# A decoder layer with 32 experts on one core: big tiles in one block by hand, another order of the front, and expert weights in pieces of 16 KB

## The chip, the cores and the metric

One core of one Trainium2 chip runs the kernel; all arithmetic is float32. The core's engines are PE (TensorE, matrix products; its weight loads are listed as PEld), DVE (VectorE), ACT (ScalarE), POOL (GpSimd) and SP (SyncE, which issues most DMAs). 16 DMA engines move the data. The metric is the time of one execution on the device in microseconds (us), the median of the runs. The profile is of one execution; its times count from the span's start, and "L122" is line 122 of the kernel.

## The reference: what is computed

One layer over 256 tokens of 1024 features:

```
proj = x @ w_in                               # 1024 -> 768 + 256
y_mix = s5_mixer(proj[:, :768])               # 48 groups of 16, 64 complex states each; GELU; GLU gate with w_glu
y_mem = cross_attention(proj[:, 768:], mem @ mem_w_k, mem @ mem_w_v)    # 4 heads, 256 memory rows
h  = layer_norm(2**0.25 * x + concat(y_mix, y_mem) @ w_out)
for each token: its 4 best of 32 experts by h @ router_w + router_b, gates = softmax of the 4 logits
expert e: g, l = split(h @ w_gu[e] + b_gu[e]);  g = min(g, 7);  l = clip(l, -7, 7)
          y_e = (g * sigmoid(1.702 * g) * (l + 1)) @ w_down[e] + b_down[e]
out = layer_norm(2**0.25 * h + sum of gate * y_e)
```

w_gu[e] is 1024 x 2048 and w_down[e] 1024 x 1024: 8.39 and 4.19 MB for each of the 32 experts, 402.65 MB in all.

## The kernel before

**The front.** x and w_in are loaded and x is transposed (xT). The S5 mixer is computed in chunks of eight tokens: DVE works out the powers of the state matrix from the small parameters (`apw`, put into PSUM as `tab`), and the function `power` (L439) forms from them three tiles m1p (input side) and three tiles m2 (output side, m20 to m22): two products on DVE into a tile and into `ptmp`, and their sum on POOL. `mats` (L214) transposes the parameters b and c from their raw layouts (`rawb`, `rawc`) for this. Out of m1p PE makes kb and, transposed by kc, the tiles tz: the products inside a chunk. ACT fills tz by copies (two from each PSUM bank of kc, and five that shift rows, for each of three blocks). u is the mixer's input; it goes through DRAM once (`ud`) to change its layout to u_sb. The state at the start of each chunk comes from a scan on DVE (`@SC1`: the rotated input through `tensor_tensor_scan`, real and imaginary part, and `@SC2`: rotated back into xs), with the table wsc that DVE builds by doubling (`@W`). `yb` sums the products inside the chunk (`@Yt`, u_sb by tz) and from the states (`@Yx`, xs by m2). Then follow GELU (`@GEL`), transposes to yT, the gate (`zp`, products with w_glu) and ymT.

Beside it runs cross-attention: mem is transposed (memT), qps, kps and vmp are the three projections, sc the scores, prob the softmax on ACT, pT its transposes and pv the product, copied to ymem (a part of `att`). `out_mem` multiplies ymem with the last quarter of w_out, and the loop at L885 multiplies ymT with the rest; all of it sums up in the four PSUM banks yp[i][hf] (i is a half of the tokens, hf a half of the features). q counts eight slices of 128 rows of w_out; slices 2 and 3 are done over all four banks, slices 4 to 7 (QO = 4) bank by bank. DVE adds the residual and takes the norm's sums, POOL raises the variance to the power -0.5, DVE normalizes, and `affine` applies gain and offset (POOL, and DVE for the last quarter). The router follows for each half i: hTp transposes, `logits`, `chosen` (the four best), ranks.

**The experts.** For expert e, `gather` (L984) makes a 0/1 matrix `oh` from ranks and multiplies the columns of h_sb (stationary, 128 of them at a time) with it: xg holds up to 64 tokens of the expert, transposed. `up` (L1014) runs eight steps kt with 128 rows of w_gu each; `act` is the clamped SwiGLU; `act_t` (L1035) transposes it in four pieces; `down` (L1044) multiplies with w_down; every second expert `combine` adds both experts' rows to `acc` by their gates. On PE the order in an expert is up, combine (every second), gather of the next expert, act_t, bias of the next, down. What would not fit in 64 slots is done by two `If` blocks behind (L1255, L1293); with these inputs they do nothing.

**Memory and loads.** A pool `big` has 22 tiles of 128 x 2048 f32 (1 MB each); a tile is handed out again when its last reader is done, and everything large lives there, weights too. `load_gu` loads 128 rows of w_gu (row kt * 128 + p to partition p, 8 KB in one piece) into one tile, `load_down` 256 rows of w_down (two pieces of 4 KB to a partition). SP issues them in the order written; an issue waits until its tile is free. Expert 31's last tile comes in two halves. At e = 22 two tiles are taken for b_down (`bd`) and the last norm's vectors.

**Order.** Instructions of PE, DVE and ACT are pinned to the order of the program (`pin`, L97; the class `Ordered`, L108). POOL and the DMA issues of SP are not: the scheduler may move them where their inputs are ready. The markers `dbg("@...")` do nothing.

Of the kernel before, what the change touches and what calls it, by code (L numbers as in the profile page):

```python
# [9 lines left out]
F32 = mybir.dt.float32  # L10
# [6 lines left out]
P = 128  # L17
# [10 lines left out]
MISS = 8192.0  # L28
NBIG = 22
# [11 lines left out]
def kernel(  # L41
# [35 lines left out]
    big = ctx.enter_context(tc.tile_pool(name="big", bufs=NBIG))  # L77
# [4 lines left out]

    def big_tile(name):
        return big.tile([P, 2048], F32, tag="big", name=name)
# [23 lines left out]
    class Ordered:  # L108
# [5 lines left out]
        def __getattr__(self, name):  # L114
            f = getattr(self.eng, name)
            return f if name == "dma_start" else lambda *a, **k: pin(f(*a, **k))  # L116

    S = Ordered(S)
    V = Ordered(V)

# [37 lines left out]
    SP.dma_start(x_sb[:, 0, :], x[0, 0:P, :])  # L158
    SP.dma_start(ldt, log_dt.rearrange("(g o) -> g o", o=1))
    SP.dma_start(araw[:, 0, :], a_re)  # L160
    SP.dma_start(araw[:, 1, :], a_im)
    SP.dma_start(x_sb[:, 1, :], x[0, P : 2 * P, :])
    win = []
    for k2 in range(4):
        t = big_tile(f"win_{k2}").rearrange("p (k n) -> p k n", k=2)
        for k in range(2):
            kt = 2 * k2 + k
            SP.dma_start(t[:, k, :], w_in[kt * P : (kt + 1) * P, :])
            win.append(t[:, k, :])
# [29 lines left out]
    )  # L199
    tt(dsk, dsk, same.unsqueeze(1).to_broadcast([P, 12, NH]), ALU.mult, G)  # L200
# [13 lines left out]
    def mats(name, in_of, a_of, b_of):  # L214
        t = big_tile(name)
        pad.append(t[:, 0 : 768 + NH])
        o = [t[:, 784 * k : 784 * k + 768].rearrange("p (g h) -> p g h", h=NH) for k in range(2)]
        for h8 in range(2):
            ps = bank(f"{name}p{h8}")
            for hh in range(8):  # L220
                tr(ps[:, NG * hh : NG * hh + NG], in_of(8 * h8 + hh), ident[0:NG, 0:NG])
            v = ps[:, 0 : 8 * NG].rearrange("p (h g) -> p g h", h=8)
            hs = slice(8 * h8, 8 * h8 + 8)
            a_of(o[0][:, :, hs], v)
            for q in range(2):
                pq, pr = slice(64 * q, 64 * q + 64), slice(64 - 64 * q, P - 64 * q)
                b_of(o[1][pq, :, hs], v[pr], pq)
        return o
# [26 lines left out]
    for kt in range(KT):  # L255
        for q in range(6):
            mm(
                ups[q // 2][:, NT * (q % 2) : NT * (q % 2) + NT], win[kt][:, P * q : P * q + P], xT[:, kt, :],
                kt == 0 and q % 2 == 0, kt == KT - 1, True,
            )  # L260
        if kt == 1:
            rbv = rawb.rearrange("g q p h -> g (q p) h")
            ba, bb_ = mats("bab", lambda h: rbv[:, :, h], lambda o, v: S.copy(o, v), lambda o, v, pq: S.copy(o, v))
        if kt == 3:
            ca, cb = mats(
                "cab", lambda h: rawc[:, h].rearrange("g q p -> g (q p)"),
                lambda o, v: S.mul(o, v, sgc), lambda o, v, pq: S.mul(o, v, sgc[pq]),
            )
            ca_pad = pad[1]
            G.memset(ca_pad[:, 768:784], 0.0)  # L270
    dbg("@LWO", None)
    wo = []
    ov = w_out[0, 0:MIX, :].rearrange("(j r) n -> r j n", r=192)

    def load_wo(k2):
        t = big_tile(f"wo{k2}").rearrange("p (k n) -> p k n", k=2)
        if k2 == 3:
            SP.dma_start(t, w_out[0, MIX:D, :].rearrange("(k p) n -> p k n", p=P))
        elif k2 < 2:
            SP.dma_start(t, ov[0:P, 2 * k2 : 2 * k2 + 2, :])  # L280
        else:
            op = ov[P:192].rearrange("r (q e) n -> e r q n", e=2)
            for e in range(2):
                SP.dma_start(t[64 * e : 64 * e + 64], op[e])
        return [t[:, 0, :], t[:, 1, :]]

    wo += load_wo(3)
# [116 lines left out]

    tab = [bank("tab0")[:, 0 : (Q + 1) * NG], bank("tab1")[:, 0 : (Q + 1) * NG]]
# [9 lines left out]
    for q in range(2):  # L415
        S.copy(bbb[64 * q : 64 * q + 64], bba[64 - 64 * q : P - 64 * q])
    dbg("apw", apw)

    dbg("@LD", None)
    mem_sb = big_tile("mem_sb").rearrange("p (m d) -> p m d", m=2)  # L420
    SP.dma_start(mem_sb, mem[0].rearrange("(m p) d -> p m d", p=P))
    wk = big_tile("wk").rearrange("p (k n) -> p k n", k=KT)
    SP.dma_start(wk, mem_w_k.rearrange("(k p) n -> p k n", p=P))
    wv = big_tile("wv").rearrange("p (k n) -> p k n", k=KT)
    SP.dma_start(wv, mem_w_v.rearrange("(k p) n -> p k n", p=P))
# [13 lines left out]
    def power(name, j, k0, m):  # L439
# [9 lines left out]
        tt(o, o, ptmp[j % 2], ALU.add, G)  # L449
# [6 lines left out]
    m1p = groups(m1p_t)  # L456

# [8 lines left out]

    dbg("@W", None)

    wsc = big_tile("wsc")
    w_re, w_im = wsc[:, 0:768], wsc[:, 768:1536]  # L470
    wre, wim = (t.rearrange("p (r c) -> p r c", c=NC) for t in (w_re, w_im))
    cv, mv_ = small("cv", (P, 2, 24)), small("mv_", (P, 24))
    for a in range(2):
        pa = slice(64 * a, 64 * a + 64)
        for o, src in ((cv[pa, 0], cs), (cv[pa, 1], sn), (mv_[pa], mag)):
            G.tensor_copy(o, src[pa].rearrange("p (r a) -> p a r", a=2)[:, a])
    e_, f_ = small("e_", (P, 2, 24)), small("f_", (P, 2, 24))
    r8 = small("r8", (P, 24, NC))
    r8f = r8.rearrange("p r c -> p (r c)")
    us = [  # L480
        u.rearrange("p (r c) -> p r c", c=NH)
        for u in (wsc[:, 1536:1920], small("u4", (P, 384)), r8f[:, 0:384], r8f[:, 384:768])
    ]
    s4 = [small(f"s4{k}", (P, 24)) for k in range(4)]

    def cmul4(o_re, o_im, x_re, x_im, y_re, y_im, t):
        yield tt(t[0], x_re, y_re, ALU.mult)
        yield tt(t[1], x_im, y_im, ALU.mult)
        yield tt(t[2], x_re, y_im, ALU.mult)
# [12 lines left out]
    while n < NC:
        b_ = [cur[:, q].unsqueeze(2).to_broadcast([P, 24, n]) for q in range(2)]
        together(
            cmul4(
                wre[:, :, n : 2 * n], wim[:, :, n : 2 * n], wre[:, :, 0:n], wim[:, :, 0:n], b_[0], b_[1],
                [u[:, :, 0:n] for u in us],
            ),
            sq(nxt, cur) if 2 * n < NC else iter(()),
        )  # L510
        n, cur, nxt = 2 * n, nxt, cur

    for _ in range(3):
        tt(mv_, mv_, mv_, ALU.mult)
# [29 lines left out]
    dbg("@KM", None)  # L544

    proj("kps", kT, lambda q, kt: wk[:, kt, P * q : P * q + P], lambda q, kt: memT[:, kt, :], (0,))
    dbg("@LG1", None)
    wgl += load_wgl(1)
    dbg("@K", None)

    kr_t = big_tile("kr")
    kr = kr_t[:, 0 : 12 * 144].rearrange("p (b n) -> p b n", b=12)
    G.memset(kr[:, :, 0:NH], 0.0)
    tz = []
    for b in range(3):
        tz.append(big_tile(f"tz{b}"))
        G.memset(tz[b], 0.0)
# [10 lines left out]
    tt(kr[:, :, NH : 2 * NH], kr[:, :, NH : 2 * NH], dsk, ALU.add, G)  # L568
# [12 lines left out]
    dbg("@M2A", None)  # L581
    m2 = groups([power("m20", 0, 1, (ca, cb))])
# [748 lines left out]
```

## Time and profile before

| what | value |
|---|---|
| median of 3 runs (lowest, highest) | 1109.77 us (1107.32, 1111.62) |
| the profiled execution | 1110.52 us, its span 1108.8 us |
| PE busy | 1056.9 us, 95% of the span |
| PE weight loads busy | 487.9 us, 44% |
| DVE, ACT, POOL busy | 285.5, 153.0, 55.6 us |
| moved by DMA | 424.75 MB, mean 383 GB/s |
| packets | 89016; under 8 KB 56180 |
| w_gu loads | 256 of 1024 KB, 19.9 us from issue to landing |
| w_down loads | 127 of 1024 KB, 20.1 us from issue to landing, and 2 of 512 KB |
| mean granted PE clock | 0.989 of full |

How to read it: matmuls are pipelined, and PE counts as busy while one is under way, so 95% does not say that PE is the limit. Which engine ends last is in the chain of waits, which is followed back from the last instruction. Where DMA loads are queued, the 20 us from issue to landing are mostly queue.

### The profile page before, as it was taken

What the parts mean: (1) busy time and instruction counts of PE and PEld (TensorE: products, weight loads), DVE (VectorE), ACT (ScalarE), POOL (GpSimd) and SP (SyncE); (2) the same over time, 40 slices, a digit from 0 to 9 for tenths busy, and PEclk for the clock granted to TensorE, in tenths of its full rate; (3) what the DMA queues carried; (4) which work ended last, traced back from release to release, by engine and by line L of the source; (5) the groups of instructions that cost most, each with busy time, mean ns of one, the idle gap of its engine ahead of it and who ended that gap; (6) DMA issues with size and microseconds to landing.
All of it is one profiled execution on the core that took longest, in us unless ns stands there. A gap on an engine that the chain in (4) does not pass through costs nothing.

```text
span 1108.8 us, 13702 instructions
## 1 busy us (share of the span) xinstructions
PE 1056.9 (95%) x5733; PEld 487.9 (44%) x5733; DVE 285.5 (26%) x632; ACT 153.0 (14%) x288; POOL 55.6 (5%) x56
## 2 busy tenths in 40 slices
PE   9988999999999999999999898989899998999994
PEld 8875654444444444444443343434243433444331
DVE  7976151121212121212121112121021212121104
ACT  4484120000000000000000000000000000011002
POOL 1750030000000000000000000000000000000001
PEclk9998999999999999999999999999999999999998
DMA  8948969999999999999999999999999999999992
GB/s 230 240 139 274 408 258 408 417 415 416 414 416 416 416 415 416 417 416 417 416 417 415 415 416 416 416 416 415 400 417 416 416 416 416 415 417 416 415 406 82
DMA packets 89016, 424.75 MB, mean 383 GB/s; under 512 B 15902, under 2 KB 18866, under 8 KB 56180
## 3 DMA queue, kind: packets, MB, share of 16 engines
q1 hardware_dynamic: 88660, 423.27, 96.1%
q8 instruction: 48, 0.79, 0.3%
q10 hardware_dynamic: 288, 0.52, 0.1%
q14 instruction: 20, 0.16, 0.0%
HBM read 421.93 MB, written 1.84 MB: 382 GB/s over the span
## 4 chain that ended last, share of the span: by engine, by line
PE 58%; DMA 37%; ACT 2%; DVE 1%; SPq 1%; issue 1%; ACTq 0%; POOL 0%; DVEq 0%
PE gu_e L122 24%; DMA gu_e<-in_exp_w_gu_dram 22%; PE dn_e L122 13%; DMA dn_e<-in_exp_w_down_dram 13%; PE xgp_e L122 7%; PE cb_e L122 4%; PE yp L122 3%; DMA win<-in_l_w_in_dram 1%; PE zp L122 1%; ACT tz L116 1%; PE atp_e L125 1%; DMA mem_sb<-in_mem_dram 1%; PE qps L122 1%; PE kps L122 1%; ACT prob L116 1%
## 5 line engine op out<-in xcount | busy, mean ns | idle before, releaser
L122 PE MATMUL gu_e<-gu_e,xg_e 128*64 128x512 f32 x2048 | 458.0, 597 | 27.0 <-DMA gu_e<-in_exp_w_gu_dram 26.3
L122 PEld LDWEIGHTS gu_e<-gu_e,xg_e 128*64 128x64 f32 x2048 | 141.9, 137 | 336.9 <-issue 253.0
L122 PE MATMUL dn_e<-dn_e,xl_te 128*64 128x512 f32 x1024 | 226.8, 595 | 0.8 <-ACT xl_te L116 0.7
L122 PEld LDWEIGHTS dn_e<-dn_e,xl_te 128*64 128x64 f32 x1024 | 70.6, 137 | 154.2 <-issue 127.7
L1028 DVE TENSOR_SCALAR xl_e<-gu_e 128x512 f32<-128x512 f32 x32 | 22.1, 692 | 430.5 <-PE gu_e L122 430.5
L122 PEld LDWEIGHTS xgp_e<-oh_e,h_sb 128*128 128x128 f32 x1024 | 118.1, 192 | 7.3 <-issue 4.3
L122 PE MATMUL xgp_e<-oh_e,h_sb 128*128 128x64 f32 x1024 | 118.2, 273 | 0.0
L1056 DVE COPY y_e<-dn_e 64x512 f32<-64x512 f32 x32 | 21.9, 684 | 252.8 <-PE dn_e L122 252.8
L116 ACT ACTIVATE sg_e<-xl_e 128x512 f32<-128x512 f32 x32 | 20.2, 630 | 405.6 <-DVE xl_e L1028 405.6
L122 PE MATMUL cb_e<-y_e,ogT_e 128*128 128x512 f32 x120 | 55.8, 604 | 0.0
L116 ACT COPY y_e<-dn_e 64x512 f32<-64x512 f32 x32 | 18.6, 582 | 257.4 <-DVE y_e L1056 250.2
L116 ACT COPY xg_e<-xgp_e 128x512 f32<-128x512 f32 x32 | 18.8, 586 | 155.5 <-PE xgp_e L122 155.5
L128 DVE TENSOR_TENSOR acc<-acc,cb_e 128x512 f32<-128x512 f32 x56 | 36.2, 681 | 6.6 <-PE cb_e L122 6.6
L122 PEld LDWEIGHTS cb_e<-y_e,ogT_e 128*128 128x128 f32 x120 | 21.6, 190 | 32.6 <-issue 29.7
L122 PE MATMUL gu_e<-bgu,ident 32*64 32x512 f32 x256 | 34.8, 612 | 0.0
L1125 POOL MEMSET bd<- 128x1280 f32 x1 | 1.2, 1165 | 583.4 <-PE gu_e L122 583.4
L131 DVE TENSOR_SCALAR oh_e<-iota,rk 128x64 f32<-128x64 f32 x62 | 12.9, 252 | 66.7 <-PE xgp_e L122 66.7
L1030 DVE TENSOR_SCALAR xr_e<-gu_e 128x512 f32<-128x512 f32 x32 | 22.1, 692 | 3.1 <-PE gu_e L122 0.2
L1031 DVE SCALAR_TENSOR_TENSOR xr_e<-xr_e,xl_e 128x512 f32<-128x512 f32 x32 | 22.0, 688 | 0.5
L122 PE MATMUL ups<-xT,win 128*128 128x256 f32 x96 | 21.7, 383 | 0.5 <-DMA win<-in_l_w_in_dram 0.5
L1032 DVE TENSOR_TENSOR xr_e<-xr_e,sg_e 128x512 f32<-128x512 f32 x32 | 21.9, 686 | 0.6 <-DVE og_e L131 0.2
L122 PE MATMUL yp<-wo,ymT 128*128 128x512 f32 x48 | 20.9, 594 | 0.0
(286 smaller groups left out, 594.8 us busy)
## 6 DMA issues: line engine op xcount, KB each, us to landing
gu_e<-in_exp_w_gu_dram SPq DMA_DIRECT2D x256, 1024.0 KB, 19.9
dn_e<-in_exp_w_down_dram SPq DMA_DIRECT2D x127, 1024.0 KB, 20.1
win<-in_l_w_in_dram SPq DMA_DIRECT2D x8, 512.0 KB, 11.0
wo<-in_w_out_dram SPq DMA_DIRECT2D x3, 1024.0 KB, 5.7
wgl<-in_l_s_w_glu_dram SPq DMA_DIRECT2D x2, 768.0 KB, 8.3
x_sb<-in_x_dram SPq DMA_DIRECT2D x2, 512.0 KB, 4.4
mem_sb<-in_mem_dram SPq DMA_DIRECT2D x1, 1024.0 KB
wk<-in_mem_w_k_dram SPq DMA_DIRECT2D x1, 1024.0 KB
```

Source lines behind the costliest of these rows:

```text
L116: return f if name == "dma_start" else lambda *a, **k: pin(f(*a, **k))
L122: pin(PE.matmul(o, lhsT, rhs, start=start, stop=stop, skip_group_check=shared))
L125: pin(PE.transpose(o, in_, ident if idn is None else idn))
L128: return (eng or V).tensor_tensor(out=o, in0=x0, in1=x1, op=op)
L131: return (eng or V).tensor_scalar(out=o, in0=x0, scalar1=s1, scalar2=s2, op0=op0, op1=op1)
L1028: V.tensor_scalar(out=xl_, in0=ps[0], scalar1=7.0, scalar2=None, op0=ALU.min)
L1030: V.tensor_scalar(out=xr, in0=ps[1], scalar1=7.0, scalar2=-7.0, op0=ALU.min, op1=ALU.max)
L1031: V.scalar_tensor_tensor(out=xr, in0=xr, scalar=1.0, in1=xl_, op0=ALU.add, op1=ALU.mult)
L1032: V.tensor_tensor(out=xr, in0=xr, in1=sg, op=ALU.mult)
L1056: eng(y[:, 512 * dh : 512 * dh + 512], ps[dh][64 * dh : 64 * dh + 64, :])
L1125: G.memset(t[:, 0:width], 0.0)
```

## The change

`big` becomes one tile of 22 slots of 2048 columns; a table `slot_of` gives each large tile of the front its slot by hand, two or more in turn in one slot. The experts' weights have a ring of blocks of two slots (ROWS = 2, 16 KB in one piece to a partition): ten blocks in slots 0 to 19, taken in the order 0 to 7, then 9, then 8. A w_gu load brings rows t * 256 + 2p and 2p + 1 to partition p (2 MB, four per expert), a w_down load rows t * 512 + 4p to 4p + 3 (2 MB, two per expert). To match, `gather` reads every second column of h_sb, and `act_t` every fourth column of the activation. SP's instructions, its DMA issues too, are now pinned to the order of the program. Expert 31's last block comes in pieces of two, one and one rows.

In the front: the small parameters are issued by ACT; the second half of x is issued right behind the first; mem, mem_w_k and mem_w_v are loaded early; rawc has another layout (q before h), and c gets its layout by matmuls with the identity instead of transposes, 2 x 2 small ones for each h; ACT's copies of it (`take_c`) come after tab and bbt. `m20` and `m21` are formed right after m1p, and m21, m22 and kr are added on DVE and not on POOL; the scan's decays r8 are made on POOL. The order of the sections changes as below. The transposed h (hT) leaves the large tiles.

```
before: ... M1A (m1p) MT UL W XQ KM K(kb, kr) M1B(m1tp) M2A KM1 SIN M2B SM(sc) kc,tz M2C SMb(max, exp) SMr
        SC1 VM VM1 PV1 SC2 Yt out_mem(1) out_mem(0) Yx GEL Z(yT) zp ...
after:  ... M1A M2(m20, m21) MT UL XQ K(kb, kr) M2C(m22) W(to 16) KM kc,tz0 KM1 SM SMb(max) W(32) tz1 M1B SIN
        exp VM VM1 SC1(real) tz2 SMr SC1(imag) Yt PV1 LX LXG SC2 Yx out_mem(1) GEL Z(yT) out_mem(0) zp ...
```

```diff
-    big = ctx.enter_context(tc.tile_pool(name="big", bufs=NBIG))
+    big = ctx.enter_context(tc.tile_pool(name="big", bufs=1)).tile([P, NBIG * 2048], F32, tag="big", name="big")
+    slot_of = {}
+    for k, names in enumerate((
+        "ptmp0 wsc", "ptmp1 gt", "m20", "m21", "m22", "u_sb", "cab s_in tw yg", "memT xs", "bbt wo3", "bab att",
+        "mem_sb wgl0", "wk wgl1", "x_sb m1p1 wgl2", "xT prob yT", "rawb m1p2 wo0", "rawc m1p0 wo1", "win_2 tz1 gb",
+        "win_3 tz2", "win_0 sv wo2", "win_1 tz0 ymT", "wv h_sb", "ut kr pT x2 acc",
+    )):
+        for name in names.split():
+            slot_of[name] = k
     def big_tile(name):
-        return big.tile([P, 2048], F32, tag="big", name=name)
+        k = slot_of[name]
+        return big[:, 2048 * k : 2048 * (k + 1)]
+    ring = [2 * k + n for k in (0, 1, 2, 3, 4, 5, 6, 7, 9, 8) for n in range(0, 2, ROWS)]
+    def next_block():
+        ring.append(ring.pop(0))
+        return big[:, 2048 * ring[-1] : 2048 * (ring[-1] + ROWS)]
...
+    SP = Ordered(SP)
...
-        tt(o, o, ptmp[j % 2], ALU.add, G)
+        tt(o, o, ptmp[j % 2], ALU.add, eng)
...
+    m2 = [power("m20", 0, 1, (ca, cb)), power("m21", 1, 1, (ca, cb), V)]
...
-    tt(kr[:, :, NH : 2 * NH], kr[:, :, NH : 2 * NH], dsk, ALU.add, G)
+    tt(kr[:, :, NH : 2 * NH], kr[:, :, NH : 2 * NH], dsk, ALU.add)
...
-    QO = 4
+    QO = 6
...
+    hv = h_sb.rearrange("p i (t r j) -> p i t j r", r=P, j=ROWS)
-                    ps[:, CAP * kt : CAP * kt + CAP], h_sb[:, i, kt * P : (kt + 1) * P], oh[:, i, :],
+                    ps[:, CAP * kt : CAP * kt + CAP], hv[:, i, kt // ROWS, kt % ROWS], oh[:, i, :],
...
+        av = a.rearrange("s (c p j) -> s c j p", p=P, j=2 * ROWS)
-            tr(ps[:, P * c : P * c + P], a[:, P * c : P * c + P])
+            tr(ps[:, P * c : P * c + P], av[:, c // (2 * ROWS), c % (2 * ROWS)])
...
-    def load_gu(n, src, kt):
-        t = big_tile(f"gu{kt}_{n}")
-        SP.dma_start(t, src[kt * P : (kt + 1) * P, :])
-        return t
+    def load_gu(src):
+        w = []
+        for t in range(KT // ROWS):
+            b = next_block().rearrange("p (j n) -> p j n", j=ROWS)
+            SP.dma_start(b, src[t * ROWS * P : (t + 1) * ROWS * P, :].rearrange("(p j) n -> p j n", j=ROWS))
+            w += [b[:, j, :] for j in range(ROWS)]
+        return w
...
+    def load_down(src, split=False):
+        n, w = 2 * ROWS, []
+        for t in range(KT // n):
+            b = next_block().rearrange("p (j n) -> p j n", j=n)
+            rows = src[t * n * P : (t + 1) * n * P, :].rearrange("(p j) n -> p j n", j=n)
...
         if e == NE - 10:
+            k = ring[0]
+            slot_of.update(bd=k, gb2=k, rows2=k + 1, o=k + 1)
+            del ring[0 : 2 // ROWS]
```

## Rows read from the trace of the kernel before

**Rows 1.** The page, part 2: GB/s that the DMA engines moved, in 40 slices of 27.7 us.
```profile
GB/s 230 240 139 274 408 258 408 417 415 416 414 416 416 416 415 416 417 416 417 416 417 415 415 416 416 416 416 415 400 417 416 416 416 416 415 417 416 415 406 82
```

**Rows 2.** The chain of waits in order of time: start us, us, what.
```profile
160.78 13.95 PE gu_e L122 x64
...
213.23 13.73 PE gu_e L122 x64
...
268.68 13.73 PE gu_e L122 x64
...
548.91 20.16 DMA dn_e<-in_exp_w_down_dram
...
1047.56 1.94 PE gu_e L122 x8
...
1065.12 8.58 PE gu_e L122 x40
```

**Rows 3.** Windows: length, busy us of each engine (instructions), granted PE clock, DMA share, GB/s.
```profile
30.00:40.00 10.00, 7.72 (x37) 6.85 (x36) 10.00 (x6) 5.24 (x7) 8.96 (x4) 0.83 1.05 374
...
620.00:624.00 4.00, 3.41 (x13) 1.16 (x12) 1.91 (x3) 0.63 (x1) 0.00 (x0) 1.00 1.02 409
632.00:644.00 12.00, 12.00 (x58) 4.02 (x56) 0.68 (x1) 0.58 (x1) 0.00 (x0) 1.00 1.01 420
...
1082.00:1087.00 5.00, 4.10 (x19) 1.66 (x19) 1.39 (x3) 0.96 (x2) 0.00 (x0) 1.00 0.46 181
...
540.00:1060.00 520.00, 493.67 (x2494) 200.67 (x2492) 92.59 (x186) 44.33 (x81) 2.12 (x2) 1.00 1.02 415
```

**Rows 4.** Timeline of SP's queue up to 215 us: start us, us, engine, line, issue, output and input.
```profile
2.67 0.42 SPq L162 DMA_DIRECT2D x_sb<-in_x_dram  x1
...
155.24 11.31 SPq L1088 DMA_DIRECT2D dn_e<-in_exp_w_down_dram  x4
167.90 17.88 SPq L1081 DMA_DIRECT2D gu_e<-in_exp_w_gu_dram  x8
```

**Rows 5.** Groups of PE weight loads: shapes, count, busy us, mean ns, idle before.
```profile
L122 PEld LDWEIGHTS xgp_e<-oh_e,h_sb 128*128 128x128 f32 x1024 | 118.1, 192 | 7.3 <-issue 4.3 <-PE cb_e L122 2.9
...
L125 PEld LDWEIGHTS babp<-ident,rawb 48*128 48x128 f32 x16 | 1.8, 203 | 0.3 <-issue 0.3
...
L125 PEld LDWEIGHTS cabp<-ident,rawc 48*128 48x128 f32 x16 | 1.1, 139 | 0.3 <-issue 0.3
```

**Rows 6.** Timeline of PE in the front: start us, us, instruction, count, idle time before it.
```profile
35.54 3.45 PE L125 MATMUL memT<-ident,mem_sb 128*128 128x128 f32 x16 [2.28 <-DMA mem_sb<-in_mem_dram]
...
49.44 2.83 PE L122 MATMUL kb<-m1p,cab 128*32 128x128 f32 x96
...
72.69 0.66 PE L125 MATMUL kc<-ident,kr 128*128 128x128 f32 x4 [2.42 <-ACT tz L116]
...
84.14 4.08 PE L125 MATMUL pTp<-ident,prob 128*128 128x128 f32 x16 [2.19 <-ACT prob L116]
88.91 3.68 PE L122 MATMUL pv<-pT,att 128*64 128x256 f32 x16 [0.69 <-ACT pT L116]
...
109.81 15.96 PE L122 MATMUL zp<-yT,wgl 128*128 128x256 f32 x96
125.69 20.87 PE L122 MATMUL yp<-wo,ymT 128*128 128x512 f32 x48
...
150.79 1.09 PE L125 MATMUL hTp<-ident,x 128*128 128x128 f32 x8
```

**Rows 7.** Timeline of DVE in the front.
```profile
39.67 5.24 DVE L116 TENSOR_TENSOR s<-cv 128x24 f32<-128x24 f32 x4
...
98.74 1.89 DVE L116 TENSOR_TENSOR xs<-tw 64x744 f32<-64x744 f32 x2
```

**Rows 8.** Timeline of ACT in the front.
```profile
76.78 3.13 ACT L116 COPY tz<-tz 32x512 f32<-32x512 f32 x5
```

**Rows 9.** Timeline of POOL in the front.
```profile
143.02 2.59 POOL L128 TENSOR_TENSOR h_sb<-x,gb 128x512 f32<-128x512 f32 x2 [0.80 <-issue]
```

More of the change, by code (lines that the diff above doesn't have):

```diff
@@ L214, in mats @@
     def mats(name, in_of, a_of, b_of):
[L215 to L217 removed]
+        banks = []
         for h8 in range(2):
@@ L287, with project @@
-    wo += load_wo(3)
+    def project(k0, k1):
+        for kt in range(k0, k1):
+            for q in range(6):
+                mm(
+                    ups[q // 2][:, NT * (q % 2) : NT * (q % 2) + NT], win[kt][:, P * q : P * q + P], xT[:, kt, :],
+                    kt == 0 and q % 2 == 0, kt == KT - 1, True,
+                )
+    project(0, 2)
+    rbv = rawb.rearrange("g q p h -> g (q p) h")
+    ba, bb_ = mats("bab", lambda h: [rbv[:, :, h]], lambda o, v: S.copy(o, v), lambda o, v, pq: S.copy(o, v))()
@@ L288 @@
+    project(2, 4)
+    take_c = mats(
+        "cab", lambda h: [rawc[:, q, h] for q in range(2)], lambda o, v: S.mul(o, v, sgc), lambda o, v, pq: S.mul(o, v, sgc[pq]),
+    )
+    project(4, 8)
     dbg("@par", None)
@@ L403 @@
         )
+    cv, mv_ = small("cv", (P, 2, 24)), small("mv_", (P, 24))
+    for a in range(2):
+        pa = slice(64 * a, 64 * a + 64)
+        for o, src in ((cv[pa, 0], cs), (cv[pa, 1], sn), (mv_[pa], mag)):
+            G.tensor_copy(o, src[pa].rearrange("p (r a) -> p a r", a=2)[:, a])
+    for _ in range(3):
+        tt(mv_, mv_, mv_, ALU.mult, G)
+    r8 = small("r8", (P, 24, NC))
+    G.tensor_copy(r8, mv_.unsqueeze(2).to_broadcast([P, 24, NC]))
+    G.memset(r8[:, :, 0], 0.0)
     tab = [bank("tab0")[:, 0 : (Q + 1) * NG], bank("tab1")[:, 0 : (Q + 1) * NG]]
@@ L543 @@
     wgl += load_wgl(0)
[L544 to L548, printed above, removed]
+    wo += load_wo(3)
     dbg("@K", None)
+    tz = [big_tile(f"tz{b}") for b in range(3)]
+    for t in tz:
+        G.memset(t, 0.0)
     kr_t = big_tile("kr")
@@ new lines @@
+    dbg("@LG1", None)
+    wgl += load_wgl(1)
+    dbg("@SM", None)
+    scores = []
+    for i in range(2):
+        sc = [bank(f"sc{i}{e}") for e in range(2)]
+        for h2 in range(2):
+            for e in range(2):
+                pe = slice(64 * e, 64 * e + 64)
+                mm(
+                    sc[e][:, NT * h2 : NT * h2 + NT], xqT[pe, h2, i * P : (i + 1) * P], kT[pe, h2, :],
+                    True, True, True,
+                )
+        scores.append(sc)
+    dbg("@SMb", None)
@@ new lines @@
+    prob = big_tile("prob").rearrange("p (i h m) -> p i h m", i=2, h=4)
+    sums = []
+    for i, sc in enumerate(scores):
+        mx, sm = small(f"mx{i}", (P, 4)), small(f"sm{i}", (P, 4))
+        for e in range(2):
+            V.tensor_reduce(
+                out=mx.rearrange("p (h e) -> p e h", e=2)[:, e, :],
+                in_=sc[e].rearrange("p (h m) -> p h m", h=2), axis=AX.X, op=ALU.max,
+            )
+        ts(mx, mx, -0.125, ALU.mult)
+        sums.append((mx, sm))
+    doubled(NC)
@@ L776 @@
             )
+    out_mem(1)
     dbg("@GEL", None)
@@ L805 @@
             )
+    out_mem(0)
     bgp = bank("bgp")
```

394 lines of the change are left out of this document (177 added, 217 removed).

## The prediction, written before the change was run

> **What bounds the kernel now.** I read the page's slices first [rows 1]: from the fifth slice but one dip, to the end, the DMA engines move 400 to 417 GB/s, and PE (TensorE) is busy for 95% of the span, so both are near a limit, and the chain of waits has to say which one ends last. It has three stretches [rows 2]. Up to 160.78 us the front runs: mixer, attention, router. From there to about 549 us the chain is PE: two experts take 268.68 - 213.23 = 55.45 us, so 27.73 each. At 548.91 it changes to DMA, and until 1047.5 one weight load follows the other. An expert's weights are 8.39 MB (w_gu) and 4.19 MB (w_down), 12.58 MB; at the 415 GB/s of that stretch [rows 3] they take 30.3 us, more than PE's 27.73. In the second stretch PE lives on a stock loaded during the front; when that is used up, DMA sets the pace. The last 61 us are PE again, released by one load.
>
> So the end is: the time at which PE begins the experts (B, 160.78), plus a short delay until its first freed tile restarts the loads, plus the bytes not yet loaded at the DMA's rate, plus a tail. At B the stock was full: the issue at 167.90 is the 25th tile, and the four before it, from 155.24 on, come singly as PE frees memory [rows 4]. Of the 22 tiles h_sb holds one, and `acc` takes none until expert 2, so 21 tiles (22.0 MB) are stock and 402.65 - 22.0 = 380.6 MB remain, 917.1 us at 415. Weights still land between 1082 and 1087 us (181 GB/s in the mean [rows 3]); some 21.5 us of PE and output follow.
>
> PE alone would end earlier, at B + 31 x 27.73 + 43.7 = 1064 us (43.7 from the last up projection's start, 1065.12 [rows 2], to the span's end). 45 us lie between the two bounds, so a faster DMA is not lost to PE before that. The front counts by B alone; loading more before B buys nothing once the ring is full.
>
> **The weights in pieces of 16 KB.** A w_gu load is 128 pieces of 8 KB, a w_down load 256 of 4 KB; both become 128 pieces of 16 KB in 2 MB. The trace has stretches of each kind alone: 420 GB/s where only 8 KB pieces run, 409 where only 4 KB pieces run [rows 3]. With 16 engines a 4 KB piece takes 4096 x 16 / 409 = 160.2 ns, an 8 KB piece 312.1. If a piece has a fixed part, that is 2 x 160.2 - 312.1 = 8.3 ns, and 16 KB take 2 x 312.1 - 8.3 = 615.9 ns: 425.6 GB/s. The mixture of the two kinds would be 416.3, and the long stretch has 415; the same loss brings 425.6 to 424.3. No weight piece of 16 KB is in the trace. Bounds: no better than 8 KB (418.7 after that loss), or no fixed part at all (303.8 ns for 8 KB, so 430.1). I take 424.3, the line through both measured lengths; a loss has a rival of its own.
>
> The ring of ten blocks holds 21.0 MB, one tile less, so 381.7 MB remain: 899.6 us (bounds 887.5 and 911.6) for 917.1: **-17.5 us**. Restart: the first block is free after two of an up projection's eight steps (3.43 us), not after one (1.72): **+1.7**. Later PE frees 12.58 MB in 27.73 us, 454 GB/s, so loads find room. Tail: the last w_gu block brings two steps at once, so PE has to do both behind it, where it now ends some 2.5 us behind the last load: **+0.9** (0 to 3).
>
> **The strided operands.** For the new row order gather reads h_sb at a step of two elements as stationary operand (32 weight loads per expert), and the activation's transposes read at a step of four (4 per expert). Weight loads bind gather: 118.1 us for 1024, 115 ns each [rows 5]. The one strided stationary operand before is rawb, at a step of 16: 1.8 us for 16 weight loads, 113 ns each, against 1.1 us (69 ns) for contiguous rawc [rows 5]. Gather's contiguous ones already take what rawb's strided ones take, so I put 0; bounds 0 and a doubling, 115 ns x 32 = 3.7 us per expert. Up to 1.9 us per expert it is hidden, DMA's 29.6 exceeding PE's 27.73, but for its share before the stock is gone, which PE has to spare.
>
> [...] No row here has a step of two.
>
> **The front**, by hand from rows 4 and 6 to 9. Gains: x's second half is issued second on SP, not at 2.67 us: -0.5. [...] c's layout takes 64 small matmul instructions instead of 16 transposes (1.1 us of weight loads [rows 5]); between 1.9 (29.5 ns each, as kb's 96 in 2.83 us [rows 6]) and twice that I take 2.6: +1.5. From kc to pv PE lost about 8 us, idle (2.42, 2.19) and slow (pTp, pv) [rows 6], all behind ScalarE. In place of that I see three waits. kr's addition moves from POOL to DVE behind m20, m21 and m21's own addition, and DVE, held 5 us at 39.67 while POOL added [rows 7], is held again: kr at about 53.5, PE ready at 50, 3.5 us. The last third of tz's copies (3.13 us on ScalarE [rows 8]) stands behind vmp's: 3.5 us before Yt. Some 1 us at pT's copies. Together 0. DVE's scans no longer stand behind reciprocals that wait for ScalarE, so xs, last written at 100.6 [rows 7], is there at about 92, in time for Yx; out_mem's 7.1 us move behind Yx, beside gelu and the copies to yT: -0.8. zp starts at 106.4 for 109.81, **-3.4**.
>
> QO = 6 gives some of it back. Half 0 of the tokens is complete 3.5 us before yp ends, not 7; POOL then does its affine (2.59 us [rows 9], and about as long again) just when the other half needs POOL for its power. The second hTp, 4.2 us after yp's end (150.79 against 146.56 [rows 6]), comes 7 us after it: **+2.8**. In SP's queue x2's loads wait for pT's memory (about 93 us), and gb and all weights stand behind them, in order; from 94 on 20 MB need 50 us, and the last block (gb's) is free at about 152 and loaded by 159, so the ring is full at B. B = 160.2, **-0.6** (bounds -8 and +8: each wait above is 3 to 5 us; two of them could go, or two more come).
>
> **Sum.** -17.5 + 1.7 + 0.9 - 0.6 = -15.5: span 1093.3. The profiled execution took 1110.52 for its span of 1108.8, 1.7 more, and stood 0.75 above the median of the runs, 1109.77. Predicted 1093.3 + 1.7 - 0.75 = 1094.2, say 1094.
>
> **Rivals.** (1) Pieces of 16 KB bring nothing over 8 KB, or are cut into shorter ones: 911.6 for 899.6, so 1106. For it: the two kinds differ by 11 GB/s only, and other causes of that are possible. Against: the longer is the faster in each stretch. Were they worse than now, 412 in the mean, it would be 926.5 and 1121. (2) The other side: the step of two slows gather's weight loads on PE. PE's bound, 160.2 + 31 x period + 43.7, passes 1108.8 from a period of 29.19 on, 46 ns more per weight load, and from there the change is slower; doubled, it is 160.2 + 31 x 31.4 + 43.7 = 1177. For it: rawb paid 44 ns. Against: a step of two, not 16, and f32 weight loads that are slow already. (3) The front is late by 8 us or more, waits stretching over a PE at its lower clock: 1102 to 1106. For it: 0.83 granted around the wait for mem_sb. (4) The front is early by 8: 1086.
>
> **How the numbers follow.** Forecast 0.62, within 1085 to 1102; rival 1 0.14 (0.04 of it the loss), rival 2 0.08, rival 3 0.09, rival 4 0.07. A measurement of this kernel can tell 0.5%, 5.5 us, from no change: faster is below 1104.2, slower above 1115.3. Faster: 0.61, rival 4 and half of rival 3, 0.72. The same: 0.10 of rival 1, the rest of rival 3 and 0.01, 0.15. Slower: rival 2, the loss and 0.01, 0.13. A range from 1082 to 1110 leaves out rival 2, the loss and the far ends.
>
> **What would show it.** About 24,600 packets of 16 KB in place of 65,500, and 424 GB/s from B on; PE's 27.73 us per expert unchanged at 200 to 500 us, gather's weight loads at 115 ns; the first up projection at 152 to 168 us; the chain changing to DMA later than at 549. It is wrong if the chain stays on PE to the end (rival 2), if the rate is 419 or less (rival 1), or if B is off by over 8 us (3, 4).

## The result

The changed kernel takes 1097.23 us (median of four runs, 1097.11 to 1097.4), the kernel before 1109.8 in the same session: a ratio of 0.9896, 95% interval 0.9876 to 0.9915. 1094 was predicted, 1082 to 1110 as the range; it is faster by more than the 0.5% that can be told from no change. The profiled span is 1095.4 us against 1108.8, so 13.4 us went; the sum had said 15.5.

The page after, part 2 and the packets' line of part 3, answers to [rows 1]. From the eighth slice on the rate is 424 to 428 GB/s, but for one dip and the end, where 414 to 417 stood; the sixth slice, in which the experts begin, has 249 for 258.

```profile
GB/s 301 128 113 284 425 249 346 427 427 426 427 425 428 428 424 428 428 425 427 427 426 427 427 427 427 427 427 425 415 426 427 427 427 428 425 427 427 426 393 56
DMA packets 43813, 424.69 MB, mean 388 GB/s; under 512 B 11311, under 2 KB 14275, under 8 KB 19173
```

The chain of waits after (start us, us, what) answers to [rows 2]. The experts begin at 164.00 instead of 160.78. Two experts take 329.01 - 273.03 = 55.98 us, 27.99 each (27.73 before). The chain changes to the loads at 691, not at 549, and leaves them at 913: from there it is TensorE's (PE's), and from 1068 on that of the closing work on the last expert's results.

```profile
164.00 13.95 PE gu_e L142 x64
...
273.03 13.73 PE gu_e L142 x64
...
329.01 13.73 PE gu_e L142 x64
...
691.35 37.74 DMA big<-in_exp_w_gu_dram
...
877.42 35.78 DMA big<-in_exp_w_gu_dram
913.24 3.65 PE gu_e L142 x16
...
1051.82 8.58 PE gu_e L142 x40
```

Windows after (length, busy us of the engines, granted PE clock, DMA share, GB/s) answer to [rows 3]: 427 in the long stretch; the last weights land behind 1070 us (20 GB/s from 1070 to 1075), not at 1087; and just before the experts PE's granted clock is 0.83 in the mean of 10 us: 0.50 from 154 to 156 us, 1.00 again from 157 on.

```profile
150.00:160.00 10.00, 8.28 (x54) 6.46 (x51) 7.13 (x22) 1.41 (x3) 4.24 (x4) 0.83 0.48 171
...
190.00:680.00 490.00, 490.00 (x2533) 211.28 (x2530) 93.00 (x191) 43.63 (x79) 0.00 (x0) 1.00 1.01 427
...
1065.00:1070.00 5.00, 5.00 (x20) 1.68 (x16) 2.54 (x4) 0.63 (x1) 0.00 (x0) 1.00 0.50 203
1070.00:1075.00 5.00, 4.09 (x21) 1.76 (x22) 0.23 (x1) 0.96 (x2) 0.00 (x0) 1.00 0.05 20
```

The old kernel in the same long stretch has 416:

```profile
190.00:680.00 490.00, 482.11 (x2506) 201.82 (x2502) 90.63 (x187) 42.20 (x77) 0.00 (x0) 1.00 1.02 416
```

The first 26 us of the experts, behind the start of the first up projection, after (first fence) and before (second):

```profile
164.00:190.00 26.00, 26.00 (x142) 11.37 (x144) 5.52 (x16) 4.74 (x9) 0.00 (x0) 1.00 0.83 337
```

```profile
160.78:186.78 26.00, 26.00 (x144) 11.19 (x146) 5.53 (x16) 4.72 (x9) 0.00 (x0) 1.00 0.97 390
```

PE's timeline in the front after answers to [rows 6]. The transposes of mem (memT) no longer wait and take 1.91 us. But the first transposes (pp) now wait for the small loads `a_re`, `a_im`, and the projection starts at 12.15 (8.70 before); zp starts at 109.33, hardly before the old 109.81; the second hTp has a new wait for VectorE (DVE), and the 16 matmuls of logits behind it take 3.23 us where the first token half's take 1.93.

```profile
6.34 0.26 PE L145 MATMUL pp<-ident,araw 48*64 48x48 f32 x1 [1.00 <-DMA araw<-in_l_s_a_re_dram]
7.40 0.37 PE L145 MATMUL pp<-ident,araw 48*64 48x48 f32 x2 [0.80 <-DMA araw<-in_l_s_a_im_dram]
...
12.15 5.96 PE L142 MATMUL ups<-big 128*128 128x256 f32 x24
...
37.78 1.91 PE L145 MATMUL memT<-ident,big 128*128 128x128 f32 x16
...
57.54 4.50 PE L145 MATMUL kc<-ident,big 128*128 128x128 f32 x24 [3.94 <-DVE big L135]
...
89.31 1.08 PE L142 MATMUL yb<-big 128*32 128x128 f32 x32 [1.72 <-ACT big L135]
...
109.33 15.96 PE L142 MATMUL zp<-big 128*128 128x256 f32 x96
125.22 20.87 PE L142 MATMUL yp<-big 128*128 128x512 f32 x48
...
147.32 1.93 PE L142 MATMUL lgp<-y_hT,wg 128*32 128x128 f32 x16
...
152.17 1.22 PE L145 MATMUL hTp<-ident,big 128*128 128x128 f32 x8 [1.73 <-DVE big L135]
...
153.88 3.23 PE L142 MATMUL lgp<-y_hT,wg 128*32 128x128 f32 x16
```

### The profile page after: what moved, and what is told of

It reads as the page before. It is cut to its first block, busy times and chain, and to the rows that moved or that the text cites. A ratio compares the mean times of both kernels' runs of the same rounds, so it can differ in the third digit from the quotient of the medians.

```text
span 1095.4 us, 13424 instructions
## 1 busy us (share of the span) xinstructions
PE 1057.1 (97%) x5781; PEld 503.2 (46%) x5781; DVE 283.1 (26%) x632; ACT 152.6 (14%) x287; POOL 44.9 (4%) x57
## 2 busy tenths in 40 slices
DMA packets 43813, 424.69 MB, mean 388 GB/s; under 512 B 11311, under 2 KB 14275, under 8 KB 19173
## 4 chain that ended last, share of the span: by engine, by line
PE 68%; DMA 16%; DVE 1%; ACT 0%; issue 0%; ACTq 0%; POOL 0%; DVEq 0%; SPq 0%
PE gu_e L142 34%; PE dn_e L142 17%; DMA big<-in_exp_w_gu_dram 12%; PE xgp_e L142 9%; PE cb_e L142 5%; DMA big<-in_exp_w_down_dram 4%; PE atp_e L145 1%; DVE big L135 0%; PE accp L142 0%; PE ogp_e L145 0%; PE lgp L142 0%; PE bc_e L142 0%; DVE st L135 0%; PE busy L142 0%; PE hTp L145 0%
## 5 line engine op out<-in xcount | busy, mean ns | idle before, releaser
L142 PE MATMUL gu_e<-big,xg_e 128*64 128x512 f32 x2048 | 448.1, 593 | 12.1 <-DMA big<-in_exp_w_gu_dram 11.2
L142 PEld LDWEIGHTS gu_e<-big,xg_e 128*64 128x64 f32 x2048 | 145.6, 137 | 308.6 <-issue 281.3
L142 PE MATMUL dn_e<-big,xl_te 128*64 128x512 f32 x1024 | 226.8, 595 | 0.7 <-ACT xl_te L135 0.7
L142 PEld LDWEIGHTS dn_e<-big,xl_te 128*64 128x64 f32 x1024 | 70.7, 137 | 154.0 <-issue 127.9
L142 PEld LDWEIGHTS xgp_e<-oh_e,big 128*128 128x128 f32 x1024 | 124.4, 196 | 7.2 <-issue 4.0
L142 PE MATMUL xgp_e<-oh_e,big 128*128 128x64 f32 x1024 | 124.4, 280 | 0.0
L148 DVE TENSOR_TENSOR big<-big,cb_e 128x512 f32<-128x512 f32 x56 | 36.1, 681 | 6.1 <-PE cb_e L142 6.1
L135 DVE TENSOR_TENSOR big<-big 128x768 f32<-128x768 f32 (+10 forms) x37 | 27.9, 763 | 15.4 <-ACT big L135 14.3
L142 PE MATMUL yp<-big 128*128 128x512 f32 x64 | 28.2, 595 | 0.0
L135 DVE TENSOR_TENSOR big<-big,tab 128x2048 f32<-128x2048 f32 x12 | 26.6, 2280 | 3.5 <-POOL big L148 3.3
```

The lines of the kernel that those rows point to most:

```text
L135: return lambda *a, **k: pin(f(*a, **k))
L142: pin(PE.matmul(o, lhsT, rhs, start=start, stop=stop, skip_group_check=shared))
L148: return (eng or V).tensor_tensor(out=o, in0=x0, in1=x1, op=op)
```

## The experiments

Each starts from the changed kernel, but for the one that starts from the kernel before. Times are medians; the kernel before stood at 1108.6 to 1110.3 beside them.

**1. Blocks of 1 MB, 8 KB pieces for both weights.**

```
-ROWS = 2
+ROWS = 1
```

> Blocks of 1 MB instead of 2 MB, 8 KB in one piece to a partition for both weights; the rest, the new front too, as in the changed kernel. Theory A (the length of the piece sets the rate: 409 GB/s at 4 KB, 420 at 8 KB, 427 at 16 KB): 381.7 MB take 908.8 us at 420 GB/s instead of 893.9 at 427, some 15 us more for the transfers, of which about 4 are hidden, because in the changed kernel TensorE ends 4 us later behind the weights than it must: 1106 to 1109 us. Rival B (the rate came from the front or from the ring and not from piece or block): 1097 us, 427 GB/s. A rival with the size of a transfer (2 MB against 1 MB) in place of the piece expects the same as A here and is told apart by the run with short pieces.

1107.77 us. 419 GB/s from 190 to 680 us, first up projection at 163.73. Theory A; the new front and ring alone give no rate. Whether it is the piece or the size of the transfer, the next experiment tells.

**2. Transfers of 2 MB, but the old row order: 8 KB and 4 KB pieces.**

```
-    ...rearrange("(p j) n -> p j n", j=ROWS)     # w_gu, and j=n for w_down
+    ...rearrange("(j p) n -> p j n", j=ROWS)
     # gather and act_t read contiguous columns again, as this order wants
```

> Transfers of 2 MB, the same blocks, ring and front as in the changed kernel, but the rows in the order of the kernel before: a partition gets 8 KB pieces of the gate and up weights and 4 KB pieces of the down weights; the gather and the transposes read contiguous columns again. Theory A (piece length): rate back to 409 GB/s in the down weights and 420 in the others, 416 in the mean, and TensorE back to 27.73 us an expert: 1110 to 1115 us (the time before, plus 3 us of the later start of the experts). Rival (the size of the transfer, 2 MB, brought the gain): 427 GB/s and 1093 to 1098 us.

1117.58 us, above A's range: 20.35 us over the changed kernel, which has the same transfers, ring and front. The size of the transfer is refuted as the cause: 2 MB transfers with the new ring and front, but without longer pieces, are 8.75 us slower than the kernel before. The window:

```profile
190.00:680.00 490.00, 478.32 (x2490) 201.27 (x2486) 90.53 (x187) 42.52 (x78) 0.00 (x0) 1.00 1.02 416
```

**3. Contiguous operands for gather and transposes**, the permutation put into the writes.

```
-                    ... hv[:, i, kt // ROWS, kt % ROWS], oh[:, i, :],
+                    ... h_sb[:, i, kt * P : (kt + 1) * P], oh[:, i, :],
+    # affine writes h_sb in that order, the activation's last product likewise
```

> Pieces of 16 KB as in the changed kernel, but the gather and the transposes of the activations read contiguous columns: the permutation is put into the writes of h and of the last product of the activation. Theory A (the step of two and four in the operands costs 6.5 ns a weight load, 0.24 us an expert, and only what lies behind the last wait for weights, five to six experts, comes to the end): gather loads back to 115 ns, 27.73 us an expert, 1095 to 1096.5 us. Rival B (TensorE bounds the whole of the experts): 31 x 0.25 us = 7.7 less, 1089 to 1090 us. Rival C (the weights bound to the end, the step is hidden): 1097 us.

1097.43 us, nothing gained: rival C, and theory A is wrong. Gather's weight loads are back to 118.1 us (first fence, after; second, this run; groups of weight loads, count, busy us), yet in PE's timeline of this run a wait appears that the changed kernel doesn't have: expert 30's last gate and up block lands at 1032.3, and PE stands 0.87 us for it. So near the end PE's bound and the loads' bound lie within 1 us of each other; what is taken from PE alone brings nothing.

```profile
L142 PEld LDWEIGHTS xgp_e<-oh_e,big 128*128 128x128 f32 x1024 | 124.4, 196 | 7.2 <-issue 4.0 <-PE cb_e L142 3.1
L145 PEld LDWEIGHTS atp_e<-ident,xr_e 128*128 128x128 f32 x128 | 19.2, 219 | 0.4 <-DVE xr_e L1078 0.4
```

```profile
L142 PEld LDWEIGHTS xgp_e<-oh_e,big 128*128 128x128 f32 x1024 | 118.1, 192 | 7.3 <-issue 4.1 <-PE cb_e L142 3.1
L145 PEld LDWEIGHTS atp_e<-ident,xl_e 128*128 128x128 f32 x128 | 15.2, 155 | 0.8 <-DVE xl_e L1086 0.8
```

```profile
1032.34 3.65 PE L142 MATMUL gu_e<-big,xg_e 128*64 128x512 f32 x16 [0.87 <-DMA big<-in_exp_w_gu_dram]
```

**4. The old order of the first loads.**

```
-    S.dma_start(ldt, ...); S.dma_start(araw[:, 0, :], a_re); S.dma_start(araw[:, 1, :], a_im)
-    SP.dma_start(x_sb[:, i, :], ...)              # i = 0, 1
+    SP.dma_start(...)                             # x_sb half 0, ldt, a_re, a_im, x_sb half 1
```

> The five first loads in the old order on SyncE's queue (first half of x, log_dt, a_re, a_im, second half of x) instead of the three small ones on ScalarE's queue and x on SyncE's; all else as in the changed kernel. Theory A (in the changed kernel the small loads land behind x, at 7.2 us, and TensorE's first transposes wait for them, 3.4 us at the first projection, which the front carries to the experts): first up at 160.5 to 161.5 us instead of 164.0, time 1093.5 to 1095 us. Rival B (the front is set later by the waits for the filter's tables and takes the 3.4 us up): first up 163 to 164 us, time 1096.5 to 1097.5 us.

1095.77 us (1094.17 to 1096.06), -1.46: between the two. The profiled run is the fastest of the four, and by itself it is theory A: 1094.17 us, first up at 160.89. Its timeline of PE shows pp without a wait and the projection 3.45 us sooner; at zp 2.24 of that is left, and at the first up projection it is 3.11 again, with the clock at 1.00 from 150 to 160 us. Where the other three lose 1.6 to 1.9 us, no trace shows.

```profile
5.27 0.32 PE L145 MATMUL pp<-ident,araw 48*64 48x48 f32 x3
...
8.70 5.42 PE L142 MATMUL ups<-big 128*128 128x256 f32 x24 [0.38 <-DMA big<-in_l_w_in_dram]
...
107.09 15.96 PE L142 MATMUL zp<-big 128*128 128x256 f32 x96
...
149.93 1.18 PE L145 MATMUL hTp<-ident,big 128*128 128x128 f32 x8 [1.73 <-DVE big L135]
```

```profile
150.00:160.00 10.00, 9.50 (x75) 8.48 (x75) 6.73 (x23) 1.36 (x3) 2.72 (x2) 1.00 0.49 175
```

**5. The old split of the output projection.**

```
-    QO = 6
+    QO = 4
```

> The last matmuls of the output projection in the old split (four of the eight inputs ahead of the passes by quarter, instead of six). Theory A (the split delays the first quarter's end, and with it the experts' start, by 2 x 4 x 4 matmuls' share, 2.8 us as the prediction took it, and a later start comes to the end in full): first up 161 to 162 us instead of 164.0, time 1094 to 1095.5 us. Rival B (the start is set elsewhere, by the stretch at a lower clock and the wait for the second half's norm): first up 163.5 to 164.5, time 1097 us.

1093.67 us, -3.56: theory A, and somewhat more than its range. The second hTp no longer waits (150.25 instead of 152.17), the clock from 150 to 160 stays at 1.00, and the first up projection starts at 160.43, 3.57 sooner; all of it reaches the end.

```profile
150.25 1.09 PE L145 MATMUL hTp<-ident,big 128*128 128x128 f32 x8
...
160.43 4.94 PE L142 MATMUL gu_e<-big,xg_e 128*64 128x512 f32 x22 [0.67 <-ACT xg_e L135]
```

```profile
150.00:160.00 10.00, 9.75 (x80) 8.71 (x76) 6.14 (x24) 1.54 (x4) 1.90 (x2) 1.00 0.95 385
```

**6. The kernel before with 8 KB pieces for w_down**, and nothing else.

```
-        rows = ...rearrange("(k p) n -> p k n", p=P)
+        rows = ...rearrange("(p k) n -> p k n", k=2)      # and act_t reads at a step of two
```

> The kernel before with one change: the down weights, still 1 MB a transfer, with two consecutive rows, 8 KB, in one piece to a partition, and the four transposes of the activations with a column step of two. Theory A (piece length alone; 416 GB/s with 4 KB and 8 KB mixed, 420 with 8 KB alone, as the run with blocks of 1 MB showed): some 359 MB between 190 us and the last wait at 420 instead of 416 GB/s, 7 to 8 us less, 1100 to 1103 us. Rival B (the larger transfers and the ring, or the front, are needed for the rate): 1107 to 1110 us.

1101.01 us, -7.62: theory A. One access pattern in the old kernel has over half of the whole change's gain. With experiment 1 (same pieces, same size of transfer) it also prices the rest of the rebuild, front and ring: 1107.77 - 1101.01 = 6.8 us worse, 3.9 of them already at the first up projection (163.73 against 159.80).

```profile
190.00:680.00 490.00, 485.76 (x2517) 206.26 (x2514) 93.97 (x193) 43.02 (x78) 0.00 (x0) 1.00 1.01 419
```

**7. The end altered.**

```
+            if e == NE - 2 and kt == 6:
+                combine(*last)                    # expert 30: ahead of its last block
+                last = None
+    # last w_gu block of experts 30, 31: one transfer for each of its two steps
```

> The changed kernel with its end altered: in expert 30 the combine of the pair before (3.63 us of TensorE) stands ahead of the last block of the gate and up weights instead of behind it, and that block of experts 30 and 31 comes in two transfers of 8 KB pieces, so that TensorE has one step of 1.8 us and not two behind the landing. Theory A (the last wait ends when that block of expert 30 lands, at 1032.3 us, and the 60 us behind it are TensorE's, 1.9 of them from the block of two steps): 3.6 + 1.8 less, of which the later transfers allow 4 to 5: 1092 to 1093.5 us. Rival B (TensorE alone bounds the end, from 913 us on, and has no idle time left in which the combine could stand): 1096.5 to 1097.5 us. Rival C (the wait moves to expert 31's blocks at once): about 1095 us.

1096.98 us: rival B. PE's timeline has no idle time around the moved combine, so nothing could be hidden in it. The profiled run begins the experts at 162.44, 1.56 us sooner than the changed kernel, and its span ends only 0.5 us sooner.

```profile
1020.62 10.47 PE L142 MATMUL gu_e<-big,xg_e 128*64 128x512 f32 x48
1031.02 3.70 PE L142 MATMUL cb_e<-y_e,ogT_e 128*128 128x512 f32 x8
1034.65 3.65 PE L142 MATMUL gu_e<-big,xg_e 128*64 128x512 f32 x16
```

**8. Parts 3, 4, 5 and 7 together**, and the combine that takes in b_down (the late one) two experts earlier, the spread of the last norm's vectors three (edits with no run of their own).

> Together: the old order of the first loads, the old split of the output projection, contiguous operands of the gather and the transposes, the late combine and the spread of the last norm's rows two experts earlier, and the altered end. Theory A (the end is the start of the experts plus the transfer of the weights at 427 GB/s plus what stands behind the last wait; the parts add): first up at 157 us, 3.6 + 3.4 + 4.5 us less than the changed kernel's 1097.2: 1085 to 1087.5 us. Rival (the two parts of the front have one and the same 3.5 us in common): 1088.5 to 1090.5 us.

1093.81 us, and all four runs, 1091.51 to 1097.26, lie above both ranges: neither the theory nor the rival. In the profiled one (1091.74) the span ends 1090.0 - 158.91 = 931.1 us after the first up projection; the changed kernel ends 931.4 after. So that run's gain is the front's alone. The two runs near 1091.6 have a mean granted clock of 0.993, the two at 1095.89 and 1097.26 have 0.989.

**9. The restart in halves.**

```
-                SP.dma_start(b, rows)             # first four blocks that are loaded again
+                SP.dma_start(b[:, j], rows[:, j]) # j = 0, 1
```

> The changed kernel, but the first four blocks that are loaded again (expert 1's down weights and the first half of expert 2's gate and up weights) come in two transfers each, 8 KB pieces, so that a half can start when TensorE is through one step of 128 rows and not two. Theory A (with 2 MB blocks the transfers stand still until TensorE has read two steps, 3.7 us behind the start of the experts instead of 1.9, and what they lose there comes to the end in full): 1.6 to 1.9 us less, 1095.3 to 1095.7 us, first transfer behind the pause 1.8 us sooner after the start of the experts. Rival (the pause is made up, or the four transfers' shorter pieces take it up): 1097 us.

1097.25 us: the rival. SP's timeline shows the restart 1.66 us sooner (166.04 for 167.70), and the windows what becomes of it: 202 GB/s for 66 from 165 to 170, but 380 for 419 from 180 to 190. PE frees the next blocks no sooner: the issues of expert 2's four blocks end at 191.0 us in both, and in the first 26 us of the experts the loads move 341 GB/s for 337.

```profile
166.04 3.76 SPq L135 DMA_DIRECT2D big<-in_exp_w_down_dram  x3
```

```profile
165.00:170.00 5.00, 5.00 (x26) 1.69 (x24) 2.31 (x9) 2.08 (x6) 0.00 (x0) 1.00 0.61 202
...
180.00:190.00 10.00, 10.00 (x61) 4.87 (x61) 0.69 (x3) 1.09 (x2) 0.00 (x0) 1.00 0.99 380
```

**10. Parts 4 and 5 alone, together.**

> Only the two parts of the front together: the old order of the first loads and the old split of the output projection; all else as in the changed kernel. Theory A (they lie on one path, one behind the other; the projections' start gave 2.2 us at the gate's matmuls, the split 3.6 at the experts' start): first up at 158 to 159 us, time 1091 to 1092.5 us. Rival (the time that the loads give is taken up by a wait further on): first up at 160 us or later, 1093 to 1094.5 us.

1091.91 us (1091.49 to 1093.76; ratio to the kernel before 0.9843, 0.9823 to 0.9864): theory A, first up at 158.17. With these two of the front's edits undone, it beats both kernels.

**11. Everything**: part 8 with the restart in halves, expert 30's combine at its second block.

> Together: the two parts of the front, the restart in halves, contiguous operands, the late combine and the spread two experts earlier, expert 30's combine between its first and second block, and the last gate and up blocks of experts 30 and 31 in halves. Theory A (end = start of the experts + transfers + what stands behind the last wait; the run with all parts but the restart ended 931.1 us behind the start, as the changed kernel does; the restart gives 1.8, the combine in an earlier wait 2): first up at 158 to 159 us, end 927 to 928 us behind it, time 1087 to 1089 us. Rival B (the altered end gives nothing again): 1089 to 1090.5 us. Rival C (with TensorE waiting more among the experts the time varies from run to run, as in the run with all parts, 1091.5 to 1097.3): above 1091 us.

1096.17 us, from 1089.47 to 1097.65: rival C, but not by its reason. The windows of the profiled run (1095.84) show a granted clock of 0.50 from 155 to 165 us, around the start of the experts and not in later waits. In the other five runs the mean granted clock goes with the time: 0.988 and 0.989 at 1096.49 to 1097.65 us, 0.994 and 0.997 at 1090.34 and 1089.47. PE's timeline shows it idle for 0.60 us at 152.9, behind DVE's strided writes of h, which take 1.08 us each (third fence; 0.70 in experiment 10, last fence):

```profile
150.00:160.00 10.00, 9.40 (x61) 8.96 (x58) 5.11 (x18) 0.28 (x2) 0.16 (x1) 0.74 0.96 377
155.00:165.00 10.00, 9.32 (x37) 6.86 (x38) 2.26 (x10) 3.64 (x7) 0.00 (x0) 0.50 0.44 184
```

```profile
153.53 2.40 PE L142 MATMUL xgp_e<-oh_e,big 128*128 128x64 f32 x16 [0.60 <-DVE lg L135]
...
157.53 3.52 PE L142 MATMUL xgp_e<-oh_e,big 128*128 128x64 f32 x16
```

```profile
150.90 2.16 DVE L135 TENSOR_TENSOR big<-big 128x512 f32<-128x512 f32 x2
```

```profile
150.48 1.41 DVE L135 TENSOR_TENSOR big<-big 128x512 f32<-128x512 f32 x2
```

**12. The same, with three matmuls on a constant in that idle stretch.**

```
     mm(rkp1[:, 0:NE], ones, msk[:, 0, :], True, False, True)
+    busy(3)
```

> The last kernel with all parts, and three more matmuls on a constant where TensorE waits for VectorE ahead of the first expert's gather (0.60 us idle at 152.9 in the trace of the run with all parts, at whose end the granted clock fell to 0.50 until 165). Theory A (the run with all parts varied between 1089.5 and 1097.6 us because this idle stretch, which the longer write of h made, drops the clock in some executions): granted clock 1.00 from 150 to 165 us, first up at 158.5 to 159.5 us, 1088.5 to 1090.5 us, and executions within 2 us of each other. Rival (the clock falls for another reason, or in the experts' waits): again 1089 to 1098 us, clock 0.50 to 0.85 somewhere in 150 to 165.

1091.44 us, 1090.95 to 1092.21 (ratio 0.9848, 0.9826 to 0.9869). Theory A in its mechanism: clock 1.00, 1.3 us between its runs where 8.2 lay, the second half of the first gather 1.97 us for 3.52, first up at 159.06. Its time is 1 us above the range. It is level with experiment 10, so the contiguous operands, the restart in halves and the altered end are worth nothing that these medians can tell. Counted from the first up projection its profiled run ends 930.4 us later, experiment 10's 931.6; of these 1.2 us the later start (159.06 for 158.17) takes 0.9 back.

```profile
155.00:165.00 10.00, 9.32 (x57) 5.24 (x58) 3.17 (x14) 3.64 (x7) 0.00 (x0) 1.00 0.76 283
```

```profile
152.85 0.91 PE L142 MATMUL busy<-ones 128*128 128x128 f32 x6
153.60 1.96 PE L142 MATMUL xgp_e<-oh_e,big 128*128 128x64 f32 x16
```

## Why the prediction was right, and where its terms were not

The mechanism was right: longer pieces, hence a faster stream, hence an earlier end. But four of its terms were mis-sized: the rate gave 5.7 us more than priced, the start of the experts took 3.8, the restart 2.2 and the end 1.8 us more. That the sum is off by only 2.1 us is luck. By the traces' packets the last weights end at 1087.4 us before and at 1071.35 after, so the spans divide as follows:

| part of the span | predicted change | measured |
|---|---|---|
| start to first up projection (B) | -0.6 | 164.00 - 160.78 = +3.2 |
| B to the last weight | -17.5 + 1.7 = -15.8 | 907.3 - 926.6 = -19.3 |
| last weight to the end | +0.9 | 24.1 - 21.4 = +2.7 |
| sum | -15.5 | -13.4 |

**Pieces (right in kind, 5.7 us too small).** The packets fell from 89016 on the page before to 43813, and the rate is 427, not 424.3: 381.7 MB take 893.9 us, not 899.6. Two things were wrong in that step. The loss of the mixture (416.3 to 415) was carried over; it was read from a long window with a dip in it (400 in [rows 1]), and from 190 to 680 us the old kernel has 416. And the fixed part is larger: 8 KB alone run at 419 (experiments 1 and 6), 312.8 ns a piece; 16 KB at 427, 613.9 ns; that leaves 2 x 312.8 - 613.9 = 11.7 ns, not 8.3, as far as a small difference of rounded rates can tell. With all other parts in place the piece's length is worth 20.35 us (experiment 2 against the changed kernel; its contiguous reads are worth nothing by experiment 3). So rival 1 is out. By the two lengths the further 8 KB of a piece take 301.1 ns, 16 x 8192 / 301.1 = 435 GB/s, an estimate of the most that still longer pieces could approach.

**The start of the experts (wrong sign, 3.8 us).** The step "x second half -0.5" moved three small loads to ScalarE's queue and counted their removal from SP's; it did not ask when they land there. They land beside the large loads, PE's transposes of them wait until 6.3 and 7.4 us, and the projection starts 3.45 us late instead of 0.5 early. At zp, 109.33 for the 106.4 of the working, 2.24 of the 2.9 are from this (experiment 4). The working's -3.4 at zp takes in 3.6 us for memT by a clock in GHz, which no run shows; the runs show its wait of 2.28 us before and none after, and its transposes in 1.91 us at a granted clock of 1.00 (37 to 40 us) for 3.45 at 0.50 (36 to 39 us), 3.8 us less together. The other steps up to there were near: c's layout +0.9 (2.07 us for 1.20; +1.5 predicted), kr's wait 3.94 (3.5 predicted), the one before Yt 1.72 (3.5 predicted). Behind yp the second hTp comes 6.1 us after yp's end (7 predicted), but from there to B pass 11.8 us, not 10: the new wait (1.73) is followed by a lower clock (0.83 from 150 to 160 us). Experiment 4 has the same wait with the clock at 1.00 and takes 160.89 - 149.93 = 11.0, experiment 5 without the wait 10.2; so about half of the 1.8 is the clock's. Experiments 4 and 5 undo the two causes one by one, experiment 10 both: 5.3 us at the end. A part of rival 3's mechanism, a wait and a lower clock behind it, was at work, at less than half its size.

**The end (1.8 us too small).** The prediction had PE catch up behind the last loads as before. With a rate of 427 the loads run ahead, and from 913 us on PE waits for none (the chain). This is not PE's strided reads: without them (experiment 3) a load sets the time at 1032.3, and the end is the same. From there to the span's end are 63.1 us, before 61.2 (from 1047.56, [rows 2]): +1.9 for the block of two steps, priced at 0.9. The weights behind that block, 16.8 MB, end 38.9 us later (at 1071.25 in experiment 3), before 39.8: another 0.9. Together that is, within 0.1, the +2.7 of the table. That PE could end sooner by waiting less was tried in experiments 7 and 8 and came to nothing.

**Restart (2.2 us too small).** In the first 26 us of the experts the loads move 337 GB/s of their later 427, 5.5 us lost; before, 390 of 416, 1.6. That is +3.9, not +1.7, and with the rate's -23.2 (893.9 - 917.1) it is the -19.3 of the table. Waiting for two steps of the first block is not what sets it: starting 1.66 us sooner changed nothing (experiment 9), since the later blocks come free no sooner.

**Strided operands (0, right for the end, not for PE).** By busy time and count, gather's weight loads went from 115.3 to 121.5 ns (118.1 and 124.4 us for 1024), the transposes' from 118.8 to 150 (15.2 and 19.2 us for 128). PE's time for an expert grew by 0.26 us (27.73 to 27.99), and experiment 3 shows that none of it reaches the end: rival 2, decided at 46 ns, got 6. It is not the step alone that counts: on the chain an expert's four transposes take 0.51 us at a step of two (experiments 1 and 6), as at the step of four (0.51 after), and 0.44 with contiguous columns (before and experiment 3). That is some 17 ns more each at either step, where gather's 32 at a step of two have 6 (3.71 us for 3.52 on the chain).

## What to carry to other kernels

Where a stream of weights bounds a kernel, give each partition its rows in one piece before anything else is rebuilt: one changed access pattern for w_down, a third of the weights (experiment 6), had 7.6 of the 12.6 us. A load that is moved to another queue must be priced by when it lands beside the large loads that now start with it, not by the slot that it frees. And when an edit is worth nothing though it does what it says, look for the second bound before taking more from the first: here PE and the loads stood within 1 us of each other near the end.

## What was not expected of the hardware

An idle stretch of 0.60 us on TensorE, ahead of a stretch that is nearly all busy, went with a fall of the granted clock to 0.50 for some 10 us (experiment 11). One execution has a trace; in the six together, 1089.47 to 1097.65 us, the mean granted clock is 0.988 to 0.990 in the four slower ones and 0.994 and 0.997 in the other two. Three matmuls without a purpose in that place held the clock at 1.00 in the traced execution and brought the four within 1.3 us. The changed kernel has a weaker form of it (0.83 from 150 to 160 us behind an idle 1.73 us), worth some 0.9 us between the second hTp and the first up projection. Experiment 4 has the same idle 1.73 us and 1.00 behind it, and so has experiment 2, with the changed kernel's own front; what decides between the two stays open.
